# Gate and up projections of a feed-forward block by Strassen's seven half-size products

## The chip, the cores and the metric

One Trainium2 chip, one core. The metric is the device time of the whole program in microseconds. Before the change three runs gave 1579.23, 1581.88 and 1583.27 us, a median of 1581.88 us.

The engines are named as the profile names them: PE multiplies matrices, DVE and POOL do elementwise work, ACT does activations and copies, SP issues the DMAs. PE's accumulators lie in PSUM (tiles `pm`), everything else in SBUF.

## The reference

The program is a mixer block followed by a second transformer block over 512 tokens of width 1024, all in float32. The change touches the feed-forward at the end of the second block alone:

```python
h = rmsnorm(x, norm_ffn_pre[l])
f = (jax.nn.silu(h @ ffn_w_gate[l]) * (h @ ffn_w_up[l])) @ ffn_w_down[l]
x = x + rmsnorm(f, norm_ffn_post[l])
```

`h` is 512 x 1024, the gate and up weights are 1024 x 2816, that is 22 column tiles of 128, and the down weights are 2816 x 1024. To keep float32 accuracy each operand a is written as a high part (a rounded to fp32r) and a low part (a minus the high part, as fp32r), and a product of two operands is three matmuls: high by high, high by low, low by high.

## The kernel before, in words

The kernel records every operation with what it reads and writes, and a list scheduler (`Recorder.schedule`) then writes out one order for each engine from a table of durations, priorities (`key`, `boost`) and the counts of free buffers. At run time each engine goes through its list in order and waits on semaphores. Operations recorded with `either` may go to one of two engines, and the scheduler chooses: `copy` between ACT and DVE, `two` and `sub` between DVE and POOL, unless an operand lies in PSUM; those stay on DVE. All of them are issued through one helper line, so the profile shows line 439 for nearly everything and tiles tell the work apart.

The activations `h`, transposed, lie in two constants: high part `hbuf` and low part `hbuf_l`, written tile of 128 tokens by tile in `norm_tile`. In the profile both are `c`; in the order rows they are `c_84` (high) and `c_85` (low).

A projection with weights as the stationary operand is `proj_b`. For two column tiles (256 columns, 1 MB) `wunit` loads the weights into `wr` (two buffers), and for each column tile makes a high part `wh` with one `copy` of 128 x 1024 and a low part `wl` with one `sub` of 128 x 1024 (three buffers each, `NWH`). Then 8 slices of K times 3 matmuls of 512 tokens each add up in one PSUM tile: 24 matmuls for one column tile. The feed-forward loop takes two column tiles of gate and the same two of up, ten times with 512-token matmuls and once, first, with each split into two halves of 256 tokens (`FFH = 2`), so that the first halves can start before the norm of the last tokens is done. ACT takes the Silu of a gate tile out of PSUM, DVE multiplies it with the up tile in PSUM, and the result is split into parts for the down projection (`split`: a `copy` and a `sub` of 128 x 512).

In what follows a pair is one turn of that loop with 512-token matmuls: two column tiles of gate and the same two of up. Here are the changed functions and what calls them.

Of the kernel before, what the change touches and what calls it, by code (L numbers as in the profile page):

```python
# [10 lines left out]
F32 = mybir.dt.float32  # L11
F32R = mybir.dt.float32r
# [8 lines left out]
NT = 4  # L21
# [470 lines left out]
def body(ctx, tc, a, out, stop=None, probe=None):  # L492
# [142 lines left out]
    def proj_a(w, c0, n, act, consume, kt=KT, tail=4, boost=0):  # L635

        hh, hl = act
        ps = {}
        group = []
        for k0 in range(0, kt, 4):
            kn = min(4, kt - k0)
            rows = slice(k0 * 128, (k0 + kn) * 128)
            src = [w[rows, c:c + m] for c, m in c0] if isinstance(c0, list) else w[rows, c0:c0 + n]
            step = 1 if tail == kt else 2
            cuts = [slice(k, min(k + step, kn)) for k in range(0, kn, step)]
            parts = wunit(src, kn, n, [(k, slice(0, n)) for k in cuts], keep=(tail == kt))  # L650
            for cut, (wh, wl) in zip(cuts, parts):
                ks = [(k0 + k, wh[:, k - cut.start, :], wl[:, k - cut.start, :]) for k in range(cut.start, cut.stop)]
                group += ks
                if k0 + cut.stop > kt - tail and k0 + cut.stop < kt:
                    continue
                for t in range(NT):
                    ts = slice(t * 128, t * 128 + 128)
                    if t not in ps:
                        ps[t] = mmp()
                    for k, h_, l_ in group:  # L660
                        first, last = k == 0, k == kt - 1
                        T.matmul(ps[t][:, :n], hh[k][:, ts], h_, start=first, stop=False)
                        T.matmul(ps[t][:, :n], hh[k][:, ts], l_, start=False, stop=False)
                        T.matmul(ps[t][:, :n], hl[k][:, ts], h_, start=False, stop=last)
                    if group[-1][0] == kt - 1:
                        rec.boost = boost
                        consume(ps[t], t)
                        rec.boost = 0
                group = []

    def split(src, hi, lo):
        copy(hi, src)
        sub(lo, src, hi)
# [10 lines left out]
    def norm_tile(t, xa, xb, g):  # L684

        xns = [t2(), t2()]
        ssq = small([128, 2], tag="ssq", bufs=4)
        for c, xc in enumerate((xa, xb)):
            ACT.activation(xns[c], xc, AF.Square, accum_out=ssq[:, c:c + 1])
        rs = small([128, 1], tag="rstd", bufs=4)  # L690
        rsqrt(rs, ssq[:, 0:1], 1.0 / D, 1e-6, 1, ssq[:, 1:2])
        for c, xc in enumerate((xa, xb)):
            xn = xns[c]
            rec.either(lambda: ACT.activation(xn, xc, AF.Copy, scale=rs),
                       lambda: V.tensor_scalar(xn, xc, rs, None, op0=OP.mult))
            ps = mxp()
            for k in range(4):
                T.transpose(ps[:, k * 128:k * 128 + 128], xn[:, k * 128:k * 128 + 128], ident)
            f = t2()
            v3 = lambda ap: ap.rearrange("p (k n) -> p k n", k=4)  # L700
            two(OP.mult, v3(f), v3(ps), g[:, 4 * c:4 * c + 4][:, :, None].to_broadcast([128, 4, 128]))
            ts = slice(t * 128, t * 128 + 128)
            split(v3(f), hbuf[:, 4 * c:4 * c + 4, ts], hbuf_l[:, 4 * c:4 * c + 4, ts])


    sp.tile([128, 448], F32, tag="pad", name="pad", bufs=1)
# [1114 lines left out]
    def post_norm(name, src, done):  # L1821

        gb = [t2(), t2()]
        for c in range(2):
            load(gb[c], bcast_rows(a[name][0][c * 512:c * 512 + 512], 512))
        ssq = [small([128, 2], tag="psq", bufs=8) for _ in range(NT)]
        o = {}

        def make(c):
            def take(ps, t):  # L1830
                o[t, c] = t2()
                ACT.activation(o[t, c], ps, AF.Square, accum_out=ssq[t][:, c:c + 1])
# [14 lines left out]
    def mixed(t, x0, x1_):  # L1847
        for c, xc in enumerate((x0, x1_)):
            load(xd[1, t * 128:t * 128 + 128, c * 512:c * 512 + 512], xc)
        norm_tile(t, x0, x1_, g3_)  # L1850

    mk = post_norm("norm_mix_post_2", xd[0], mixed)
    for c in range(2):
        proj_a(a["w_out_2"][0], c * 512, 512, (mh, ml), mk(c), tail=TAIL2 if c else 4, boost=NBOOST * c)


    NF = 22
    fh, fl = [], []
    for j0 in range(0, NF, 2):
        sg_ = {}  # L1860

        def take_g(ps, j):
            sg_[j] = t2()
            ACT.activation(sg_[j], ps, AF.Silu)

        def take_up(ps, j):
            two(OP.mult, sg_[j], sg_[j], ps)
            fh.append(t2(F32R))
            fl.append(t2(F32R))
            split(sg_[j], fh[-1], fl[-1])  # L1870

        proj_b(a["ffn_w_gate_2"][0], j0 * 128, 256, hact, take_g, parts_of=2 if j0 < FFH else 1)
        proj_b(a["ffn_w_up_2"][0], j0 * 128, 256, hact, take_up, parts_of=2 if j0 < FFH else 1)

    def finish(t, x0, x1_):
        for c, xc in enumerate((x0, x1_)):
# [30 lines left out]
```

## Time and profile before

| | us |
|---|---|
| median of three runs | 1581.88 |
| the profiled execution's own time | 1583.61 |
| its span | 1581.8 |
| PE busy | 1475.5 (93%) |
| DVE busy | 1040.0 (66%) |
| ACT busy | 416.0 (26%) |
| POOL busy | 377.6 (24%) |

Busy shares are averages over stages with different limits. The feed-forward fills the last 370 us of the span: the two half-token tiles from about 1209 us, the ten pairs from about 1232 us to 1450 us, and the down projection with the last norm after that. In this stage the granted clock is 1.00, the upper of the two levels (2.4 GHz). Two things help in reading the rows below. An instruction's duration in the trace runs a little into the next one on the same engine, so the spacing of starts is the rate of an engine that is kept fed, and it is shorter than the duration. And an instruction that cannot get what it needs from the memory shows as a longer duration, not as an idle gap, so waits of that kind count as busy time.

### The profile page before, as it was taken

The numbers are of one execution on the slowest core, as the hardware profiler recorded it, in microseconds if no ns is written. First come the engines' busy times: TensorE is split into PE (matmuls) and PEld (weight loads), VectorE is DVE, ScalarE is ACT, GpSimd is POOL, SyncE is SP. The second block draws the span as 40 slices with busy tenths as digits, with TensorE's granted clock in tenths as the row PEclk, the third lists the DMA queues.
The fourth block names the chain that finished last, engine by engine and source line by source line (L and its number), as shares of the span: only waits on it lengthen the run. The fifth ranks groups of instructions, "written<-read, shape, count | busy, mean of one in ns | idle before, by whom it ended". The sixth has DMA issues, their size and how long they took to land.

```text
span 1581.8 us, 19335 instructions
## 1 busy us (share of the span) xinstructions
PE 1475.5 (93%) x7092; PEld 1210.0 (76%) x7092; DVE 1040.0 (66%) x2130; ACT 416.0 (26%) x905; POOL 377.6 (24%) x439
## 2 busy tenths in 40 slices
PE   6895988688999999989999999999999999999997
PEld 5674766577788887878887777778888888888886
DVE  5999995798874696696444777874478434443444
ACT  4351324344321132252011534431114111111010
POOL 2788741441200123020001221232120111110000
PEclk9997999899999999999999999999999999999999
DMA  8614232255613222213323223213343323333232
GB/s 235 203 40 156 82 79 51 67 149 180 213 49 127 62 78 83 81 35 99 106 81 120 94 67 105 69 54 106 118 151 118 106 88 99 107 96 104 81 133 107
DMA packets 169455, 165.26 MB, mean 104 GB/s; under 512 B 36992, under 2 KB 136200, under 8 KB 169232
## 3 DMA queue, kind: packets, MB, share of 16 engines
q1 hardware_dynamic: 169360, 164.02, 33.1%
q8 instruction: 56, 0.92, 0.2%
q14 instruction: 39, 0.32, 0.1%
HBM read 150.64 MB, written 10.47 MB: 102 GB/s over the span
## 4 chain that ended last, share of the span: by engine, by line
PE 65%; DVE 13%; DMA 2%; issue 2%; ACT 1%; POOL 1%; SPq 0%; DVEq 0%; ACTq 0%; POOLq 0%
PE pm L439 65%; DVE t L439 9%; DVE s L439 2%; DVE wl L439 1%; ACT t L439 1%; DMA wr<-w_in 1%; DMA wr<-w_ada 1%; POOL t L439 1%; DVE wh L439 1%; DVE c L439 0%; DMA t<-t 0%; SPq L439 0%; DMA t<-gla_w_alpha 0%; ACT L439 0%; ACT s L439 0%
## 5 line engine op out<-in xcount | busy, mean ns | idle before, releaser
L439 PE MATMUL pm<-c,wh 128*128 128x512 f32 (+1 forms) x1952 | 568.9, 388 | 4.5 <-DVE wh L439 2.5
L439 PEld LDWEIGHTS pm<-c,wh 128*128 128x128 f32 x1952 | 359.1, 189 | 75.5 <-DVE wh L439 3.4
L439 POOL TENSOR_TENSOR t<-t,t 128x512 f32<-128x512 f32 (+11 forms) x282 | 261.7, 941 | 627.7 <-ACT t L439 421.2
L439 DVE CAST wh<-wr 128x1024 fp32r<-128x1024 f32 x160 | 113.9, 712 | 356.4 <-PE pm L439 344.2
L439 PE MATMUL pm<-c,wl 128*128 128x512 f32 (+1 forms) x976 | 325.5, 387 | 0.6 <-DVE wl L439 0.5
L439 ACT ACTIVATE t<-pm 128x512 f32<-128x512 f32 (+8 forms) x315 | 150.1, 502 | 510.9 <-PE pm L439 488.0
L439 PE MATMUL pm<-t,t 128*128 128x256 f32 (+4 forms) x1232 | 242.3, 324 | 30.9 <-DVE t L439 18.2
L439 DVE TENSOR_TENSOR wl<-wr,wh 128x1024 fp32r<-128x1024 f32 (+2 forms) x195 | 244.1, 1255 | 24.3 <-PE pm L439 9.3
L439 PEld LDWEIGHTS pm<-t,t 128*128 128x128 f32 (+1 forms) x1232 | 193.7, 191 | 62.8 <-issue 14.2
L439 PEld LDWEIGHTS pm<-c,wl 128*128 128x128 f32 x976 | 183.1, 189 | 36.8 <-DVE wl L439 1.4
L439 PE MATMUL pm<-wh,c 128*128 128x512 f32 (+1 forms) x576 | 177.6, 391 | 4.0 <-DVE wh L439 2.5
L439 PE MATMUL pm<-c,t 128*128 128x128 f32 (+4 forms) x638 | 123.7, 307 | 30.9 <-DVE t L439 14.7
L439 PE MATMUL pm<-wh,t 128*128 128x512 f32 x480 | 142.2, 390 | 0.3 <-POOL t L439 0.3
L439 ACT ACTIVATE t<-t 128x512 fp32r<-128x512 f32 (+6 forms) x140 | 79.0, 581 | 229.2 <-DVE t L439 168.3
L439 PE MATMUL pm<-t,wh 128*128 128x512 f32 x416 | 137.2, 391 | 0.0
L439 PEld LDWEIGHTS pm<-c,t 128*128 128x128 f32 (+3 forms) x638 | 82.8, 152 | 64.2 <-issue 16.2
L439 PEld LDWEIGHTS pm<-wh,c 128*128 128x128 f32 x576 | 108.3, 192 | 26.9 <-DVE wh L439 3.2
L439 POOL TENSOR_TENSOR wl<-wr,wh 128x1024 fp32r<-128x1024 f32 (+1 forms) x17 | 42.7, 2513 | 320.6 <-DVE wh L439 200.6
L439 PE MATMUL pm<-wl,c 128*128 128x512 f32 (+1 forms) x288 | 104.6, 394 | 15.0 <-DVE wl L439 15.0
L439 ACT ACTIVATE wh<-wr 128x1024 fp32r<-128x1024 f32 (+2 forms) x52 | 52.9, 1019 | 203.9 <-PE pm L439 149.6
L439 PEld LDWEIGHTS pm<-wh,t 128*128 128x128 f32 x480 | 90.0, 188 | 20.0 <-POOL t L439 0.7
L439 DVE TENSOR_TENSOR t<-pm,t 64x256 f32<-64x256 f32 (+8 forms) x157 | 85.2, 557 | 24.8 <-ACT t L439 17.8
(113 smaller groups left out, 1346.4 us busy)
## 6 DMA issues: line engine op xcount, KB each, us to landing
wr<-w_in SPq DMA_DIRECT2D x48, 1024.0 KB, 5.0
wr<-w_branch SPq DMA_DIRECT2D x12, 1024.0 KB, 5.2
wr<-ffn_w_gate SPq DMA_DIRECT2D x11, 1024.0 KB, 5.2
wr<-ffn_w_up SPq DMA_DIRECT2D x11, 1024.0 KB, 5.2
wr<-ffn_w_down SPq DMA_DIRECT2D x10, 1024.0 KB, 5.0
wa<-w_ada SPq DMA_DIRECT2D x32, 256.0 KB, 4.3
wr<-w_out SPq DMA_DIRECT2D x8, 1024.0 KB, 4.9
wr<-w_in SPq DMA_DIRECT2D x12, 512.0 KB, 3.8
```

The lines of the kernel that those rows point to most:

```text
L439: self.rec.record(self.eng, lambda: fn(*args, **kw), writes, reads, self.duration(name, writes, reads, kw))
```

## The change

For 20 of the 22 column tiles (all but the first two) the product of 1024 x 256 weights with 512 tokens is split into 2 x 2 blocks: K in halves of 512, columns in halves of 128, tokens in halves of 256. Seven products of half-size blocks (Strassen, in Winograd's form) replace eight. Each of the seven has a stationary operand of 4 slices of K by 128 columns and a moving operand of 256 tokens, and is again three matmuls for each slice of K: 7 x 4 x 3 = 84 matmuls of 256 tokens for two column tiles instead of 48 of 512.

Of the weight blocks, four combinations are formed in place in `wr` (`two`, 128 x 512 each), and each of the seven operands gets its own high and low part, both in one tile (`block`: a `copy` and a `sub` of 128 x 512). Of the activations, four combinations with their parts are formed once (`combine`, called after the half-token tiles). The seven products come back from PSUM through seven DVE operations that add them up. The product of Silu(gate) and up, `glu_half`, is now of two SBUF tiles, and its split into parts is recorded after all pairs.

```diff
+    def block(src):
+        tag = ("wh", "wl")[blocks[0] % 2]
...
+        hi, lo = (t[:, c:c + 512].rearrange("p (k n) -> p k n", k=4) for c in (0, 512))
+        copy(hi, src)
+        sub(lo, src, hi)
...
+        def product(o, wp_, b):
+            for k in range(4):
+                T.matmul(o, wp_[0][:, k, :], b[k][0], start=(k == 0), stop=False)
+                T.matmul(o, wp_[0][:, k, :], b[k][1], start=False, stop=False)
+                T.matmul(o, wp_[1][:, k, :], b[k][0], start=False, stop=(k == 3))
...
+            w11 = block(a11)
+            product(x[:, lo_], w11, b11)
+            two(OP.subtract, a21, a11, a21)
+            ws3 = block(a21)
+            two(OP.subtract, a21, a22, a21)
+            ws2 = block(a21)
+            two(OP.add, a11, a11, a21)
+            ws1 = block(a11)
+            product(y[:, lo_], ws3, t3)
+            product(x[:, hi_], ws2, t2_)
+            product(y[:, hi_], ws1, t1)
+            w12 = block(a12)
+            w22 = block(a22)
+            two(OP.subtract, a12, a12, a21)
+            ws4 = block(a12)
+            product(z[:, lo_], w12, b21)
+            product(z[:, hi_], w22, t4n)
+            product(q[:, lo_], ws4, b22)
+            copy(o[:, lo_], x[:, lo_])
+            V.tensor_tensor(m[:, lo_], o[:, lo_], x[:, hi_], op=OP.add)
+            V.tensor_tensor(m[:, hi_], m[:, lo_], y[:, lo_], op=OP.add)
+            V.tensor_tensor(h2(p), h2(m), y[:, None, hi_].to_broadcast([128, 2, 256]), op=OP.add)
+            V.tensor_tensor(o[:, lo_], o[:, lo_], z[:, lo_], op=OP.add)
+            V.tensor_tensor(o[:, hi_], m[:, hi_], z[:, hi_], op=OP.add)
+            V.tensor_tensor(p[:, lo_], p[:, lo_], q[:, lo_], op=OP.add)
...
-        proj_b(a["ffn_w_gate_2"][0], j0 * 128, 256, hact, take_g, parts_of=2 if j0 < FFH else 1)
-        proj_b(a["ffn_w_up_2"][0], j0 * 128, 256, hact, take_up, parts_of=2 if j0 < FFH else 1)
...
+            proj_s(a["ffn_w_gate_2"][0], j0 * 128, 256, hact, comb, take_g2)
+            proj_s(a["ffn_w_up_2"][0], j0 * 128, 256, hact, comb, lambda os, j: [glu_half(sg_[z], os[z]) for z in range(2)])
```

The scheduler settles the order on each engine. In the middle of the ten pairs DVE's list before reads as follows; `wr_2436` and `wr_2445` are the raw weights of one pair's gate and up, and these ten rows are the whole pair:

```order
L439 CAST wh_2437<-wr_2436 128x1024
L439 TENSOR_TENSOR wl_2438<-wr_2436,wh_2437 128x1024
L439 CAST wh_2439<-wr_2436 128x1024
L439 TENSOR_TENSOR t_2422<-t_2422,pm_2430 128x512
L439 TENSOR_TENSOR wl_2440<-wr_2436,wh_2439 128x1024
L439 CAST wh_2446<-wr_2445 128x1024
L439 TENSOR_TENSOR t_2424<-t_2424,pm_2433 128x512
L439 TENSOR_TENSOR wl_2447<-wr_2445,wh_2446 128x1024
L439 CAST wh_2448<-wr_2445 128x1024
L439 TENSOR_TENSOR wl_2449<-wr_2445,wh_2448 128x1024
```

After the change a pair has 35 rows on DVE, and the same 35 come back pair by pair. These twelve are a third of one pair (`wr_2466` is its gate, `wr_2481` its up; `wh_2467` is the operand w11 of the gate, `wh_2473`, `wl_2474` and `wh_2477` are ws2, ws1 and ws4; `pm_2453` to `pm_2456` are the products of the unit before):

```order
L439 TENSOR_TENSOR wr_2466<-wr_2466 128x4x128
L439 TENSOR_TENSOR t_2465<-t_2465,pm_2454 128x256
L439 TENSOR_TENSOR wh_2467<-wr_2466,wh_2467 128x512
L439 TENSOR_TENSOR t_2464<-t_2465,pm_2454 128x512
L439 TENSOR_TENSOR wr_2466<-wr_2466 128x4x128
L439 TENSOR_TENSOR wr_2481<-wr_2481 128x4x128
L439 CAST wh_2477<-wr_2466 128x512
L439 TENSOR_TENSOR t_2463<-t_2463,pm_2455 128x256
L439 TENSOR_TENSOR wh_2477<-wr_2466,wh_2477 128x512
L439 TENSOR_TENSOR wh_2473<-wr_2466,wh_2473 128x512
L439 TENSOR_TENSOR wl_2474<-wr_2466,wl_2474 128x512
L439 TENSOR_TENSOR t_2463<-t_2465,pm_2455 128x256
```

The whole 35 are 18 operations of two SBUF inputs on 128 x 512 (combinations of weights, low parts, one product with Silu, one low part of the result), 4 casts of 128 x 512, 2 sums of 128 x 512 and 10 of 128 x 256 with one input in PSUM, and one copy of 128 x 256 out of PSUM.

On POOL a pair had two rows before, the low parts of two result tiles. These are two pairs and a half:

```order
L439 TENSOR_TENSOR t_2432<-t_2422,t_2431 128x512
L439 TENSOR_TENSOR t_2435<-t_2424,t_2434 128x512
L439 TENSOR_TENSOR t_2452<-t_2442,t_2451 128x512
L439 TENSOR_TENSOR t_2455<-t_2444,t_2454 128x512
L439 TENSOR_TENSOR t_2472<-t_2462,t_2471 128x512
```

After the change it has eight: three combinations of weights, three low parts of weight blocks, one product with Silu and one low part of a result:

```order
L439 TENSOR_TENSOR wr_2466<-wr_2466 128x4x128
L439 TENSOR_TENSOR wh_2475<-wr_2466,wh_2475 128x512
L439 TENSOR_TENSOR wr_2466<-wr_2466 128x4x128
L439 TENSOR_TENSOR wl_2476<-wr_2466,wl_2476 128x512
L439 TENSOR_TENSOR t_2448<-t_2448,t_2463 128x512
L439 TENSOR_TENSOR wh_2487<-wr_2481,wh_2487 128x512
L439 TENSOR_TENSOR t_2691<-t_2449,t_2690 128x512
L439 TENSOR_TENSOR wr_2481<-wr_2481 128x4x128
```

All eight read two SBUF tiles. ACT has 15 rows in a pair where it had four: eleven high parts of weight blocks, two Silu, one copy out of PSUM and one high part of a result. On PE the operand w11 of a unit is taken between the last two products of the unit before: the order of a boundary is (`wh_2461` and `wl_2462` are w22 and ws4 of the unit before)

```order
L439 MATMUL pm_2455<-t_2365,wh_2461 128x256
L439 MATMUL pm_2468<-c_84,wh_2467 128x256
L439 MATMUL pm_2468<-c_85,wh_2467 128x256
L439 MATMUL pm_2455<-t_2364,wh_2461 128x256 x2
L439 MATMUL pm_2455<-t_2365,wh_2461 128x256
L439 MATMUL pm_2456<-c_84,wl_2462 128x256
L439 MATMUL pm_2455<-t_2364,wh_2461 128x256
L439 MATMUL pm_2468<-c_84,wh_2467 128x256 x2
```

## Rows read from the trace of the kernel before

**Rows 1.** The page: span, and busy time of each engine with its instructions.
```profile
span 1581.8 us, 19335 instructions
PE 1475.5 (93%) x7092; PEld 1210.0 (76%) x7092; DVE 1040.0 (66%) x2130; ACT 416.0 (26%) x905; POOL 377.6 (24%) x439
```

**Rows 2.** The chain that ended last: start, us, what; the feed-forward's stretch.
```profile
1209.34 9.40 PE pm L439 x77
1218.79 0.64 PE pm L439 x4
...
1221.59 349.64 PE pm L439 x1595
1571.25 0.70 ACT t L439 x2
```

**Rows 3.** Busy time in stretches: us, engines (instructions), granted clock, DMA share, GB/s.
```profile
1254.00:1276.00 22.00, 22.00 (x99) 18.21 (x98) 8.87 (x10) 2.46 (x4) 3.08 (x2) 1.00 0.32 96
1364.00:1386.00 22.00, 22.00 (x99) 18.22 (x98) 8.87 (x10) 2.46 (x4) 3.08 (x2) 1.00 0.30 96
```

**Rows 4.** PE in order of time, start and us: 512-token matmuls late in the pairs.
```profile
1441.51 0.61 PE L439 MATMUL pm<-c,wh 128*128 128x512 f32 x2
...
1449.24 0.39 PE L439 MATMUL pm<-c,wl 128*128 128x512 f32 x1
```

**Rows 5.** PE in order of time: 256-token matmuls of the half-token tiles.
```profile
1210.03 0.40 PE L439 MATMUL pm<-c,wh 128*128 128x256 f32 x2
...
1213.51 0.40 PE L439 MATMUL pm<-c,wh 128*128 128x256 f32 x2
```

**Rows 6.** DVE in order of time, undisturbed: 512 columns, 256 out of PSUM, a cast.
```profile
411.95 0.42 DVE L439 CAST t<-wr 128x512 fp32r<-128x512 f32 x1
412.33 4.05 DVE L439 TENSOR_TENSOR t<-wr,t 128x512 fp32r<-128x512 f32 x3
...
538.53 0.42 DVE L439 TENSOR_TENSOR t<-pm,t 128x256 f32<-128x256 f32 x1
538.87 0.42 DVE L439 BATCH_NORM_STATS2 s<-pm 128x6 f32<-128x256 f32 x1
...
1208.60 0.68 DVE L439 TENSOR_TENSOR c<-t,c 128x512 fp32r<-128x512 f32 x1
1209.20 0.68 DVE L439 TENSOR_TENSOR t<-pm,c 128x512 f32<-128x512 f32 x1
```

**Rows 7.** DVE in order of time, where POOL works at the same time.
```profile
860.93 1.28 DVE L439 SCALAR_TENSOR_TENSOR t<-t,pm 128x512 f32<-128x512 f32 x2
...
1079.11 1.22 DVE L439 TENSOR_TENSOR wl<-wr,wh 128x1024 fp32r<-128x1024 f32 x1
1080.73 1.83 DVE L439 TENSOR_TENSOR wl<-wr,wh 128x1024 fp32r<-128x1024 f32 x1 [0.40 <-ACT wh L439]
...
1162.89 1.63 DVE L439 CAST wh<-wr 128x1024 fp32r<-128x1024 f32 x1
```

**Rows 8.** POOL in order of time, in the same moments, and back to back.
```profile
123.10 4.62 POOL L439 TENSOR_TENSOR t<-t,t 128x512 f32<-128x512 f32 x4
...
859.90 3.26 POOL L439 TENSOR_TENSOR wl<-wr,wh 128x1024 fp32r<-128x1024 f32 x1 [0.69 <-PE pm L439]
...
1079.28 2.20 POOL L439 TENSOR_TENSOR t<-t,t 128x512 f32<-128x512 f32 x1 [13.82 <-DVE t L439]
...
1161.83 2.13 POOL L439 TENSOR_TENSOR t<-t,t 128x512 f32<-128x512 f32 x1 [12.52 <-DVE t L439]
```

**Rows 9.** Groups by form from 1230 to 1440 us: count, busy us, mean ns.
```profile
L439 DVE TENSOR_TENSOR wl<-wr,wh 128x1024 fp32r<-128x1024 f32 x38 | 46.5, 1223 | 1.9
L439 POOL TENSOR_TENSOR t<-t,t 128x512 fp32r<-128x512 f32 x20 | 30.4, 1519 | 229.0 <-ACT t L439 229.0
...
L439 ACT ACTIVATE t<-t 128x512 fp32r<-128x512 f32 x20 | 12.7, 633 | 107.3 <-DVE t L439 107.3
```

More of the change, by code (lines that the diff above doesn't have):

```diff
@@ L656, in proj_a @@
                 for t in range(NT):
-                    ts = slice(t * 128, t * 128 + 128)
+                    tok = lambda x: x[t] if isinstance(x, list) else x[:, t * 128:t * 128 + 128]
                     if t not in ps:
@@ L661, in proj_a @@
                         first, last = k == 0, k == kt - 1
-                        T.matmul(ps[t][:, :n], hh[k][:, ts], h_, start=first, stop=False)
-                        T.matmul(ps[t][:, :n], hh[k][:, ts], l_, start=False, stop=False)
-                        T.matmul(ps[t][:, :n], hl[k][:, ts], h_, start=False, stop=last)
+                        T.matmul(ps[t][:, :n], tok(hh[k]), h_, start=first, stop=False)
+                        T.matmul(ps[t][:, :n], tok(hh[k]), l_, start=False, stop=False)
+                        T.matmul(ps[t][:, :n], tok(hl[k]), h_, start=False, stop=last)
                     if group[-1][0] == kt - 1:
@@ new lines, in combine @@
+    def combine(f):
+        tiles = [[(t2(F32R), t2(F32R)) for _ in range(2)] for _ in range(4)]
+        v3 = lambda ap: ap.rearrange("p (k n) -> p k n", k=4)
+        for q in range(2):
+            t1, t2_, t3, t4n = (t2() for _ in range(4))
+            two(OP.subtract, t1, f[q + 2][0], f[q][0])
+            two(OP.subtract, t3, f[q + 2][1], f[q + 2][0])
+            two(OP.subtract, t2_, f[q + 2][1], t1)
+            two(OP.subtract, t4n, f[q][1], t2_)
+            for z, src in enumerate((t1, t2_, t3, t4n)):
+                for kp in range(2):
+                    hi, lo = (x.rearrange("p (k n) -> p k n", k=2)[:, :, q * 128:q * 128 + 128] for x in tiles[z][kp])
+                    split(v3(src)[:, 2 * kp:2 * kp + 2, :], hi, lo)
+        return [[tuple(x[:, k % 2 * 256:k % 2 * 256 + 256] for x in z[k // 2]) for k in range(4)] for z in tiles]
@@ L686, in norm_tile @@
         xns = [t2(), t2()]
+        fs = []
         ssq = small([128, 2], tag="ssq", bufs=4)
@@ L703, in norm_tile @@
             split(v3(f), hbuf[:, 4 * c:4 * c + 4, ts], hbuf_l[:, 4 * c:4 * c + 4, ts])
+            fs.append(f)
+        return fs
     sp.tile([128, 448], F32, tag="pad", name="pad", bufs=1)
@@ L1849, in mixed @@
             load(xd[1, t * 128:t * 128 + 128, c * 512:c * 512 + 512], xc)
-        norm_tile(t, x0, x1_, g3_)
+        ftok[t] = norm_tile(t, x0, x1_, g3_)
+    ftok = {}
     mk = post_norm("norm_mix_post_2", xd[0], mixed)
@@ L1857, in body, with glu_half @@
     NF = 22
-    fh, fl = [], []
+    ff = []
+    def glu_half(g, u):
+        two(OP.mult, g, g, u)
+        ff.append(g)
     for j0 in range(0, NF, 2):
@@ L1864, in take_g, with take_g2, f_slices @@
             ACT.activation(sg_[j], ps, AF.Silu)
[L1866 to L1870, printed above, removed]
-        proj_b(a["ffn_w_gate_2"][0], j0 * 128, 256, hact, take_g, parts_of=2 if j0 < FFH else 1)
-        proj_b(a["ffn_w_up_2"][0], j0 * 128, 256, hact, take_up, parts_of=2 if j0 < FFH else 1)
+        def take_g2(os, j):
+            for z, o in enumerate(os):
+                ACT.activation(o, o, AF.Silu)
+                sg_[z] = o
+        if j0 < FFH:
+            proj_b(a["ffn_w_gate_2"][0], j0 * 128, 256, hact, take_g, parts_of=2)
+            proj_b(a["ffn_w_up_2"][0], j0 * 128, 256, hact, lambda ps, j: glu_half(sg_[j], ps), parts_of=2)
+            if j0 + 2 == FFH:
+                comb = combine(ftok)
+        else:
+            proj_s(a["ffn_w_gate_2"][0], j0 * 128, 256, hact, comb, take_g2)
+            proj_s(a["ffn_w_up_2"][0], j0 * 128, 256, hact, comb, lambda os, j: [glu_half(sg_[z], os[z]) for z in range(2)])
+    fp = []
+    for f in ff:
+        fp.append((t2(F32R), t2(F32R)))
+        split(f, *fp[-1])
+    def f_slices(x):
+        res = []
+        for j in range(NF):
+            if j < FFH:
+                res.append([fp[j][x][:, t * 128:t * 128 + 128] for t in range(NT)])
+            else:
+                res.append([fp[j - j % 2 + t // 2][x][:, j % 2 * 256 + t % 2 * 128:j % 2 * 256 + t % 2 * 128 + 128]
+                            for t in range(NT)])
+        return res
+    fh, fl = f_slices(0), f_slices(1)
     def finish(t, x0, x1_):
```

26 lines of the change are left out of this document (added).

## The prediction

> **What bounds the kernel now.** I read the page first, then the chain of waits, then stretches of the feed-forward, then single instructions in order of time.
>
> The page has PE busy in 93% of a span of 1581.8 us, DVE in 66%, ACT and POOL in about a quarter [rows 1]. The chain says more: from 1221.59 to 1571 us it is PE alone, 1595 matmuls without a link through another engine [rows 2]. So in the stage that the change touches PE sets the end, and what PE saves there is saved. The stretches agree: in 22 us, which is about one pair of gate and up, PE is busy for 22.00, DVE for 8.87, POOL for 3.08, ACT for 2.46, at a granted clock of 1.00, the upper level [rows 3]. The reader should see how much room DVE and POOL have there; the question is whether the change needs more than that room.
>
> **The change part by part.**
>
> *PE.* Late in the pairs 34 matmuls of 512 tokens start between 1441.51 and 1449.24 us, 0.227 us each [rows 4]. The half-token tiles have 29 matmuls of 256 tokens between 1210.03 and 1213.51 us, 0.120 us each, with the same 128 x 128 stationary operands [rows 5]. So half the tokens cost a little more than half. Removed are 20 x 48 = 960 of the first kind, 217.9 us; added are 20 x 84 = 1680 of the second, 201.6 us. PE's own saving is 16.3 us, not the eighth of 218 that counting multiplications would give. In pairs: 96 x 0.227 = 21.8 us before, 168 x 0.120 = 20.2 us after.
>
> The Trainium skill, "TensorE: Matmul & The Clock Gate", section "Back-to-back issue gap", gives a warm isolated gap of N/2.4 + 2.5 ns, 216 and 109 ns here. By that the saving would be 960 x 0.216 - 1680 x 0.109 = 24 us, an estimate from the page; the trace has 227 and 120 ns, which decide.
>
> *DVE.* Undisturbed and kept fed, a two-input operation of 128 x 512 starts 0.60 us before the next (1208.60 to 1209.20), one of 128 x 256 out of PSUM 0.34 (538.53 to 538.87), a cast of 128 x 512 0.38 (411.95 to 412.33) [rows 6]. The 35 rows of a pair are then 18 x 0.60 = 10.8 (two SBUF inputs), 4 x 0.38 = 1.5 (casts), 2 x 0.60 = 1.2 and 11 x 0.34 = 3.7 (out of PSUM), together 17.2 us where there were 8.9. By itself this fits into 20.2 us of PE.
>
> *POOL.* A pair has eight operations of 128 x 512 instead of two. Four back to back take 4.62 us [rows 8], under 1.2 us each; eight are some 9 us. This fits too.
>
> *Both together.* They cannot run at the same time. At 1079.28 us POOL starts an operation 0.17 us into a DVE subtraction that takes its usual 1.22 us to 1080.33; POOL's takes 2.20, to 1081.48: it waited for DVE and then ran for 1.15. The next DVE subtraction starts at 1080.73 and takes 1.83 instead of 1.22, because POOL was still at work for 0.75 [rows 7 to 9]. The cast at 1162.89 lost even more, 1.63 us beside a POOL operation that ended at 1163.96. Only the two DVE operations at 860.93 with an input in PSUM keep to 0.64 each, in the middle of a POOL operation of 3.26 us [rows 7, 8]. So each POOL operation of 128 x 512 blocks a DVE operation with two SBUF inputs, or an SBUF cast, for 1.0 to 1.1 us, and is blocked by it in turn.
>
> The Trainium skill, "SBUF — State Buffer", section "Who interferes with whom", states the same as a rule: DVE's second read port is GpSimd's, the pair of ports is an exclusive lock held for the whole instruction, and a DVE instruction with at most one SBUF input outside the two-port modes does not take it. It speaks against this change, which puts both engines on that lock; the trace agrees with it, at 1.22 against 1.83 us and at 0.64 us undisturbed.
>
> The sum for the lock in a pair: 10.8 + 1.5 us of DVE and 8 x 1.0 to 1.1 us of POOL, 20.3 to 21.1 us. This is as long as PE's 20.2 even when the 4.9 us of DVE work out of PSUM lies entirely beside POOL. It won't, since DVE runs its list in order. Where a POOL operation gets in beside one operation of 0.34 us, DVE loses 0.65 us.
>
> A second limit: the operand ws4 of a unit takes the buffer of w11 of the same unit (every second operand has the same tag, three buffers). The order has the cast of ws4 three rows behind w11's low part, and it waits until PE has finished w11, which stands interleaved with the last two products of the unit before. From w11's first low part PE has about 25 matmuls to go, 3.0 us, and 0.2 us for the signals; the three rows between are 1.8 us. So DVE idles for 1.4 us twice in a pair, 2.8 us. During these idles and the row out of PSUM beside them four of the eight POOL operations can run for nothing (their inputs are ready then). The other four cost 4 x 0.65 = 2.6 us. An operation started afresh takes 0.68 instead of 0.60 us, eight times, 0.6 us. Together 17.2 + 2.8 + 2.6 + 0.6 = 23.2, and I take 23.3 us for a pair, 1.5 more than before, 15 us in ten pairs. The bounds are 20.2 (PE alone, -16) and 26 us (17.2 and eight holds of 1.1 that nothing hides, +42).
>
> *The start.* Four combinations of the activations and their parts need eight subtractions of 128 x 512 and sixteen casts and subtractions each of 128 x 256, about 8 x 0.6 + 16 x 0.7 = 16 us spread over three engines, in the time in which before DVE finished the norm of the last tokens and PE waited for it (from 1218.79 to 1221.59 us in the chain [rows 2]). POOL takes six of the early ones, in the midst of DVE's chain of small operations for that norm. I charge 2 us for the norm and 3 us for the second up tile of the half-token stage, whose weights DVE now prepares behind nineteen other rows: 5 us, bounds 0 and 10.
>
> *What costs nothing.* ACT goes from 4 to 15 operations in a pair, 15 x 0.63 = 9.5 us [rows 9], below any of the others. The weights loaded are the same megabyte for each unit, at a DMA share of 0.3 [rows 3]. The down projection and the last norm keep their work; the parts of the results are made one pair later than before, well ahead of use.
>
> The sum against the profiled execution, 1583.6 us: + 15 + 5 = 1603.6. That execution lay 1.7 us above the median of the runs, so I predict 1602 us; alone this case has 1592 to 1614.
>
> **The rivals.**
>
> *PE stays the bound.* It needs DVE and POOL to pass the lock back and forth almost without loss, 20.2 us in a pair. For it: each of the engines alone has room, and six operands can be ready ahead of PE. Against it: the lock alone needs at least as long. The time: 1583.6 - 16.3 + 2 - 1.7 = 1568 us. (By the page's gaps on PE it would be 8 us less.)
>
> *The lock, well packed.* POOL's operations all meet DVE's idle time or its work out of PSUM: a pair of 21.1 to 21.8 us, -7 to 0 us in ten, with 3 to 5 us at the start: about 1580 us. For it: DVE has 4.9 us out of PSUM and 2.8 us idle for POOL's 8 to 8.8 us. Against it: POOL's operations become ready together, after the same DVE row.
>
> *The lock, badly packed.* Nearly every hold falls on DVE, and PE's late products then hold up DVE's sums: a pair of 25 to 26 us, +32 to +42, with 5 to 8 at the start: about 1626 us. The point from which it decides is DVE without idle time and POOL waiting on DVE's last row, which three of its eight operations do by their inputs.
>
> **How the numbers follow.** My forecast has a chance of 0.60, PE as the bound 0.13, the well packed lock 0.13, the badly packed 0.14. A change under 0.3% (4.7 us) can't be told from none. Faster by more: all of the PE case and a little of the well packed one, 0.15. Within: most of the well packed one, 0.10. Slower: the rest, 0.75. The range is 1572 to 1628 us: it leaves out most of the PE case and the upper end of the badly packed one, and holds the bounds of the start.
>
> **What would show it.** In the stretch of the pairs PE should be busy for less than nine tenths where it had no idle time, with its waits on DVE's and POOL's low parts (`wh`, `wl`); DVE should be busy for over nine tenths; its subtractions of 128 x 512 beside POOL should average over 0.8 us where those out of PSUM stay at 0.69; ten pairs should take some 233 us. Idle PE under 3% in the pairs, or subtractions that keep to 0.69 us beside POOL, would prove the lock harmless and me wrong. If the first pair starts at the time it did before, the 5 us for the start are wrong.

## The result: 2.97% slower, and the profile after

The changed kernel takes 1629.32 us (median of four runs, 1624.83 to 1631.36) where the kernel before, run beside it, takes 1582.14 us: a ratio of 1.0297 with an interval of 1.0271 to 1.0323. The forecast was 1602 us with a range of 1572 to 1628. Its direction was right, and so was the cause that it named, DVE and POOL shutting each other out; the step by which half of POOL's operations cost nothing failed, and the change cost 47 us in place of 20. Times here and below are medians of the fast runs, without one slow run each of e6 and e8. In the profiled execution the page has, as answer to [rows 1] (span; busy time, share and instructions of each engine):

```profile
span 1626.5 us, 21349 instructions
PE 1477.3 (91%) x7812; PEld 1240.4 (76%) x7812; DVE 1207.3 (74%) x2396; ACT 483.8 (30%) x1025; POOL 487.5 (30%) x513
```

No engine looks full here: a page is a mean over stages. The second stretch of [rows 3], and a longer one that is used below to compare kernels (us; each engine's busy time and instructions; granted clock; DMA share; GB/s):

```profile
1364.00:1386.00 22.00, 19.03 (x151) 18.22 (x152) 21.36 (x30) 6.90 (x13) 11.55 (x8) 1.00 0.32 98
...
1270.00:1410.00 140.00, 117.86 (x923) 112.39 (x923) 136.16 (x193) 48.38 (x83) 67.09 (x45) 0.99 0.27 83
```

PE, which was busy for 22.00 of 22 us, is now busy for 19.03; DVE went from 8.87 to 21.36. Over 140 us DVE is busy for 97% and PE for 84%: the bound has moved to DVE. DVE's list for one pair, from one first eviction (`COPY t<-pm`) to the next, in order of time (start, duration, instruction, and in brackets what ended an idle time before it):

```profile
1340.96 0.41 DVE L439 COPY t<-pm 128x256 f32<-128x256 f32 x1
1341.30 0.67 DVE L439 TENSOR_TENSOR wl<-wr,wl 128x512 fp32r<-128x512 f32 x1
...
1343.16 1.73 DVE L439 TENSOR_TENSOR wh<-wr,wh 128x512 fp32r<-128x512 f32 x1
1344.81 0.67 DVE L439 TENSOR_TENSOR t<-t,pm 128x512 f32<-128x512 f32 x1
1345.41 1.78 DVE L439 TENSOR_TENSOR wr<-wr 128x512 f32<-128x512 f32 x2
1347.82 0.43 DVE L439 CAST wh<-wr 128x512 fp32r<-128x512 f32 x1 [0.63 <-PE pm L439]
...
1350.96 1.68 DVE L439 TENSOR_TENSOR wl<-wr,wl 128x512 fp32r<-128x512 f32 x1
1352.57 1.78 DVE L439 TENSOR_TENSOR t<-t,t 128x512 f32<-128x512 f32 x1
...
1355.87 1.45 DVE L439 TENSOR_TENSOR wr<-wr 128x512 f32<-128x512 f32 x1
...
1357.84 1.77 DVE L439 TENSOR_TENSOR wh<-wr,wh 128x512 fp32r<-128x512 f32 x1
1359.54 1.77 DVE L439 TENSOR_TENSOR wr<-wr 128x512 f32<-128x512 f32 x1
...
1363.70 1.77 DVE L439 TENSOR_TENSOR wh<-wr,wh 128x512 fp32r<-128x512 f32 x1
...
1366.39 0.41 DVE L439 COPY t<-pm 128x256 f32<-128x256 f32 x1
```

And POOL's list for the same time, in the same columns:

```profile
1343.05 1.29 POOL L439 TENSOR_TENSOR wr<-wr 128x512 f32<-128x512 f32 x1 [3.56 <-DVE wr L439]
1344.29 1.75 POOL L439 TENSOR_TENSOR wl<-wr,wl 128x512 fp32r<-128x512 f32 x1
1350.79 1.30 POOL L439 TENSOR_TENSOR t<-t,t 128x512 f32<-128x512 f32 x1 [4.75 <-DVE t L439]
1352.30 1.50 POOL L439 TENSOR_TENSOR wh<-wr,wh 128x512 fp32r<-128x512 f32 x1 [0.20 <-ACT wh L439]
1355.09 1.68 POOL L439 TENSOR_TENSOR t<-t,t 128x512 fp32r<-128x512 f32 x1 [1.29 <-ACT t L439]
1357.39 3.37 POOL L439 TENSOR_TENSOR wr<-wr 128x512 f32<-128x512 f32 x2 [0.63 <-DVE wr L439]
1363.58 1.34 POOL L439 TENSOR_TENSOR wh<-wr,wh 128x512 fp32r<-128x512 f32 x1 [2.81 <-ACT wh L439]
```

A pair takes 25.43 us (1340.96 to 1366.39). The rows at 1341.30 and 1344.81 show what a two-input operation of 128x512 takes when nothing blocks it, 0.67 to 0.68 us. Eight rows are longer, each beside one of POOL's eight operations: by 1.05, 0.50 (1.78 for two instead of 1.28), 1.00, 1.10, 0.77, 1.09, 1.09 and 1.09 us, together 7.7 us, 0.96 each. Such a lengthening is called a hold below. DVE is idle once, for 0.63 us. The rest, 25.43 - 7.7 - 0.63 = 17.1 us, is DVE's own work. The row at 1344.81 reads PSUM and runs at 0.67 us in the midst of a POOL operation (1344.29 to 1346.04).

The pair is 25.43 - 21.8 = 3.6 us longer than before, 36 us in ten pairs. The rest of the 47 us is lost at the start, in the half-token tiles. Executions differ by a few us ahead of the changed stage already, so the start is counted from a mark in the unchanged part, PE's 5300th matmul (it starts at 1188.07 us before and 1186.71 after), to the first matmul on gate and up weights behind the 192 of the half-token tiles (1236.85 and 1245.27): 48.8 us before, 58.6 after, 9.8 lost. From there to the end of the span it is 345.0 and 381.3 us, 36.3 more. DVE in the norm of the last tokens:

```profile
1214.90 0.16 DVE L439 SCALAR_TENSOR_TENSOR s<-s,s 128x1 f32<-128x1 f32 x1
...
1216.38 0.87 DVE L439 SCALAR_TENSOR_TENSOR s<-s,s 128x1 f32<-128x1 f32 x1
...
1217.78 1.25 DVE L439 SCALAR_TENSOR_TENSOR s<-s 128x1 f32<-128x1 f32 x1
```

POOL at that time, six subtractions of the token combinations in a row:

```profile
1215.95 7.20 POOL L439 TENSOR_TENSOR t<-t,t 128x512 f32<-128x512 f32 x6 [7.06 <-DVE t L439]
```

And PE, which waits for the norm's result:

```profile
1223.58 1.37 PE L439 MATMUL pm<-c,t 128*128 128x128 f32 x8 [4.56 <-DVE t L439]
1225.68 1.01 PE L439 MATMUL pm<-c,wh 128*128 128x256 f32 x3 [0.74 <-ACT c L439]
1228.33 0.58 PE L439 MATMUL pm<-c,wh 128*128 128x256 f32 x1 [1.64 <-DVE c L439]
...
1234.26 0.37 PE L439 MATMUL pm<-c,wl 128*128 128x256 f32 x1
```

A row of one column, 0.16 us when free, takes 0.87 and 1.25 us beside POOL, and the norm is a chain of such rows; rows of the combinations stand between them in DVE's own list too. PE goes on with the last tokens at 1228.33 us; before it was at 1221.59 [rows 2], 6.7 us earlier. After these waits 27 matmuls of 256 tokens start between 1228.33 and 1234.26, 0.220 us each in place of 0.120 [rows 5], 2.7 us more, with the granted clock at its lower level, 0.50, for four of the microseconds:

```profile
1229.00:1233.00 4.00, 4.00 (x21) 4.00 (x21) 4.00 (x7) 0.72 (x2) 2.93 (x3) 0.50 0.01 4
...
1245.00:1253.00 8.00, 6.04 (x45) 5.84 (x44) 6.53 (x7) 2.31 (x4) 3.81 (x3) 0.91 0.08 19
```

The second line is the first Strassen tile, where PE is idle for another 2.0 us; that lies inside the first pair, which takes 25.2 us, no longer than the others, and is not a loss of the start. The late resumption (6.7 us, 8.1 by the mark) and the lower clock (2.7 us) are the 9.8 us of the start to within 1 us.

### The profile page after: what moved, and what is told of

It is laid out like the page before. It is cut to its first block, busy times and chain, and to the rows that moved or that the text cites. A ratio compares the mean times of both kernels' runs of the same rounds, so it can differ in the third digit from the quotient of the medians.

```text
span 1626.5 us, 21349 instructions
## 1 busy us (share of the span) xinstructions
PE 1477.3 (91%) x7812; PEld 1240.4 (76%) x7812; DVE 1207.3 (74%) x2396; ACT 483.8 (30%) x1025; POOL 487.5 (30%) x513
## 4 chain that ended last, share of the span: by engine, by line
PE 53%; DVE 24%; issue 3%; DMA 2%; POOL 1%; ACT 1%; SPq 0%; DVEq 0%; ACTq 0%; POOLq 0%
PE pm L439 53%; DVE t L439 13%; DVE wl L439 4%; DVE wh L439 3%; DVE s L439 2%; POOL t L439 1%; DVE wr L439 1%; ACT t L439 1%; DMA wr<-w_in 1%; DMA wr<-w_ada 1%; DVE c L439 1%; DMA t<-t 0%; SPq L439 0%; DMA t<-gla_w_alpha 0%; POOL wh L439 0%
## 5 line engine op out<-in xcount | busy, mean ns | idle before, releaser
L439 PE MATMUL pm<-c,wh 128*128 128x512 f32 (+1 forms) x1672 | 484.4, 368 | 15.2 <-DVE wh L439 11.0
L439 PEld LDWEIGHTS pm<-c,wh 128*128 128x128 f32 x1672 | 303.3, 192 | 63.5 <-DVE wh L439 13.7
L439 DVE CAST wh<-wr 128x1024 fp32r<-128x1024 f32 (+1 forms) x132 | 92.2, 699 | 230.1 <-PE pm L439 220.8
L439 PE MATMUL pm<-t,wh 128*128 128x256 f32 (+1 forms) x896 | 234.2, 334 | 2.0 <-DVE wh L439 2.0
L439 PE MATMUL pm<-t,wl 128*128 128x256 f32 (+1 forms) x688 | 170.4, 319 | 6.5 <-DVE wl L439 6.5
L439 ACT ACTIVATE wh<-wr 128x512 fp32r<-128x512 f32 (+1 forms) x110 | 89.4, 814 | 281.9 <-PE pm L439 224.9
L439 PEld LDWEIGHTS pm<-t,wh 128*128 128x128 f32 x896 | 155.0, 191 | 19.5 <-DVE wh L439 3.2
L439 ACT ACTIVATE t<-t 128x512 f32<-128x512 f32 (+6 forms) x162 | 89.3, 572 | 161.6 <-DVE t L439 96.3
L439 PEld LDWEIGHTS pm<-t,wl 128*128 128x128 f32 x688 | 117.8, 193 | 16.0 <-DVE wl L439 8.0
L439 DVE TENSOR_TENSOR t<-t,t 128x512 f32<-128x512 f32 (+8 forms) x174 | 124.8, 729 | 7.0 <-DMA t<-t 2.1
```

Of the source, the lines that this page charges most:

```text
L439: self.rec.record(self.eng, lambda: fn(*args, **kw), writes, reads, self.duration(name, writes, reads, kw))
```

## The experiments

The texts set apart, written before each run, say TensorE, VectorE, GpSimd and ScalarE for PE, DVE, POOL and ACT. The theory at the beginning: each of the eight POOL operations of a pair locks DVE out for some 0.97 us, and this makes DVE the bound at 25.4 us. Rival A: DVE is held up by PE, which gives weight blocks back too late (the step with 2.8 us of idle time in the prediction). Rival B: PE's stream of 256 tokens is slower than was charged.

A pair is 168 matmuls, so matmuls in the stretch from 1270 to 1410 us give the pair: 923 of them are 25.5 us (and 25.43 from eviction to eviction). Ratios are to the kernel before, run beside it.

| version | POOL operations a pair | pair, us | time, us | ratio |
|---|---|---|---|---|
| changed kernel | 8 | 25.5 | 1629.3 | 1.0297 (1.0271 to 1.0323) |
| e1 ScalarE copies in place of POOL | 0 | 20.1 | 1576.3 | 0.9971 (0.9958 to 0.9985) |
| e2 more POOL | 12 | 26.3 | 1642.0 | 1.0382 (1.0363 to 1.0401) |
| e3 DVE alone | 0 | 20.1 | 1579.8 | 0.9988 (0.9979 to 0.9998) |
| e4 combinations off POOL | 8 | 25.8 | 1621.9 | 1.0250 (1.0233 to 1.0267) |
| e6 e3 and e4 | 0 | 20.8 | 1575.3 | 0.9971 (0.9960 to 0.9983) |
| e7 e6 and norm first | 0 | 20.6 | 1571.7 | 0.9950 (0.9938 to 0.9963) |
| e8 half of POOL's | 4 | 24.3 | 1606.8 | 1.0167 (1.0151 to 1.0182) |
| e9 e7 and casts on ScalarE | 0 | 20.1 | 1566.6 | 0.9915 (0.9902 to 0.9929) |
| e10 holds alone | 4 | 23.2 | 1606.7 | 1.0161 (1.0144 to 1.0178) |
| e11 e8, four blocks | 5 | 21.0 | 1589.5 | 1.0056 (1.0041 to 1.0071) |
| e12 changed, four blocks | 10 | 24.0 | 1617.8 | 1.0224 (1.0204 to 1.0244) |

### e1: the same lists, without POOL

Operations recorded within the pairs and the splits of their products are marked (`zone`); the planner's order stays.

```diff
+        rec.ops[-1].subst = lambda: nc.scalar.activation(dst, a_, AF.Copy)      # in two()
...
-                op.call()
+                (op.subst if op.zone and op.subst and op.eng == "POOL" else op.call)()
```

> In the twenty Strassen tile pairs and the splits of their products, each two-input operation that GpSimd had (about 83, eight in a gate-and-up pair) is replaced by a ScalarE copy of its first input, so the weight differences and low parts that GpSimd made are not computed; VectorE and TensorE run the same lists as in the changed kernel. Theory (the lock on SBUF between VectorE and GpSimd makes VectorE the bound, eight holds of 0.97 us a pair): the pair falls from 25.4 to 20.2 to 20.6 us, where TensorE is next (VectorE's own 35 rows are 17.2), and the time to 1577 to 1584 us. Rival A (VectorE waits for TensorE to give back weight blocks, whatever GpSimd does): only the 0.6 us idle a pair and a little latency go, pair above 24, time 1610 to 1625. Rival B (TensorE's 256-wide stream is slower than the 0.120 us charged): pair 22 to 24, time 1595 to 1615.

The stretch 1270 to 1410 us in its trace:

```profile
1270.00:1410.00 140.00, 140.00 (x1169) 140.00 (x1168) 120.63 (x243) 88.42 (x159) 0.00 (x0) 1.00 0.33 103
```

PE is busy for all of the 140 us, 0.120 us a matmul: rival B falls, PE's term of the prediction is right. The pair and the time (1576.3 us) came out just under the theory's ranges. The groups by form in 1260 to 1420 us (count; busy us, mean ns; idle time before them and what ended it) show DVE's rows free of stalls, and its waits for PE:

```profile
L441 DVE TENSOR_TENSOR wh<-wr,wh 128x512 fp32r<-128x512 f32 x39 | 26.1, 685 | 0.4
...
L441 DVE CAST wl<-wr 128x512 fp32r<-128x512 f32 x16 | 6.8, 427 | 11.6 <-PE pm L441 11.6
...
L441 DVE CAST wh<-wr 128x512 fp32r<-128x512 f32 x8 | 3.4, 426 | 9.4 <-PE pm L441 9.4
```

The first of these groups in the changed kernel, between 1270 and 1410 us:

```profile
L439 DVE TENSOR_TENSOR wh<-wr,wh 128x512 fp32r<-128x512 f32 x28 | 35.8, 1297 | 0.0
```

Its mean falls from 1297 to 685 ns. DVE waits 21.0 us for PE in 160 us, 2.6 us a pair. That is the idle time which the prediction put at 2.8. It is there when PE is the bound and nothing blocks DVE.

### e3: GpSimd taken out, arithmetic whole

```diff
-        if not any(in_psum(view(x)) for x in (dst, a_, b_)):
+        if not rec.zone and not any(in_psum(view(x)) for x in (dst, a_, b_)):      # in two(): no POOL in the pairs
```

> The same arithmetic, with GpSimd taken out of the pairs: its eight operations go to VectorE. Theory (lock): VectorE has 17.2 + 8 x 0.60 = 22.0 us of rows a pair and no stalls; pair 22.0 to 22.6, time 1629 - 31 = 1598 us (1594 to 1604). Rival A (VectorE is late by its own work and by waits for TensorE): eight more rows on the bound engine, pair 25.4 + 4.8 = 30, time 1677; Rival B (TensorE's stream): pair stays at 24 to 25.4, time 1615 to 1630.

```profile
1270.00:1410.00 140.00, 140.00 (x1169) 140.00 (x1169) 137.70 (x262) 73.08 (x129) 0.00 (x0) 1.00 0.33 104
```

DVE has more to do than in the changed kernel, 19.8 us a pair in place of 17.1, and the pair became 5.3 us shorter: rival A in its form "DVE has too much to do" is out. With e1, where the lists are the same, it is POOL's part that costs the time; e10 below separates its holds from its slowness. The size was missed by 18 us. The pair is not 22.0 us but PE's 20.1, because the planner made another list. In the groups from 1260 to 1420 us DVE has nine casts of weights, about one a pair in place of three, and only two of the subtractions that split the products, which are put off until after the pairs:

```profile
L441 DVE CAST wl<-wr 128x512 fp32r<-128x512 f32 x5 | 2.1, 424 | 0.1
L441 DVE CAST wh<-wr 128x512 fp32r<-128x512 f32 x4 | 1.7, 425 | 0.1
L441 DVE TENSOR_TENSOR t<-t,t 128x512 fp32r<-128x512 f32 x2 | 1.4, 684 | 0.0
```

DVE has 137.70 us of 140 to do, just less than PE. In all the kernel is within 0.3% of the one before: what the pairs win (16 us) is lost again outside them. By the mark the start takes 57.9 us in place of 48.8, 9.1 of it; where the down projection begins PE stands for another 1.95 us (1453.76 to 1455.71), waiting for `wh`.

### e4, e6, e7, e9: the start

e4 keeps the pairs as they are and takes POOL out of the combinations alone; e6 is e3 and e4; e7 also lets no combination start before the norm of all tokens; e9 also puts every cast in the pairs and combinations on ACT.

```diff
+                rec.zone = True                     # e4, e6, e7, e9
+                rec.after = tuple(normed)           # e7, e9: all operations of the norm come first
                 comb = combine(ftok)
+                rec.after = ()
...
+        if rec.zone:                                # e9, in copy()
+            ACT.activation(dst, src, AF.Copy)
+            return
```

> Only the token combinations ahead of the pairs are kept off GpSimd (their differences and low parts run on VectorE); the pairs are as in the changed kernel. Theory (the start's 7 us comes from GpSimd's holds on the small VectorE rows of the last tokens' norm): the last tokens' c_85 is ready some 4 us earlier, VectorE has some 3 us more of its own work, time 1622 to 1628 us. Rival (the combinations themselves are late, whoever does them): same or later, 1629 to 1633.

> GpSimd is kept off both the pairs and the token combinations; the arithmetic is whole. Theory (two separate costs of the same lock, the pairs' and the start's): the gains of the two single edits add, 1580 - 7 = 1573 us (1570 to 1576), pair 20.16 us as TensorE sets it. Rival (with the pairs bound by TensorE the start's gain is lost again, since VectorE has the combinations to do itself): 1577 to 1582.

> As the run before, and the combinations may start only when the norm of all four token tiles is done. Theory (VectorE's order at the start, combinations between the small rows of the last norm, keeps TensorE waiting for the last tokens): TensorE resumes at about 1218 us in place of 1222 to 1225, time 1569 us (1565 to 1572). Rival (the combinations are then late for the first pair, which waits for them): 1573 to 1580.

> As the norm-first version, with every cast of the pairs and combinations on ScalarE (before, the planner chose VectorE for some). Theory (TensorE is the bound at 20.16 us a pair, and VectorE at 19.8 has just enough room): VectorE falls to some 19 us a pair and the time stays within 2 us of the norm-first version. Rival (VectorE still holds TensorE back here and there): 3 to 6 us faster than that version.

e4 won 7.5 us, a little more than was expected. PE goes on with the last tokens at 1221.75 us, 6.6 us earlier; 2.0 of that lie ahead of the stage (the 5300th matmul starts at 1184.76). By the mark the start takes 54.4 us in place of 58.6, so POOL's holds there cost 4.2 of the 9.8 us, net of the work that DVE took over.

e6 came to 1575.3, near the upper end of what the two gains added give. e7 won another 3.7 us, resumes with the last tokens at 1219.89 us and came to 1571.7, inside its range; by the mark its start takes 48.8 us, as in the kernel before. Of the other 5.6 of the start's 9.8 us, 1.9 go with POOL out of the pairs too (e6, 52.5 us) and 3.7 when the combinations no longer stand ahead of the norm's last rows in DVE's list.

In e6 and e7 PE is not quite full in the pairs: 1129 and 1144 matmuls between 1270 and 1410 us make 20.8 and 20.6 us a pair. In e6 that is a single pair of 25.0 us, with a wait of 2.31 us for DVE and a granted clock of 0.78 from 1385 to 1390 us behind it; in e7 each pair from 1316 us on takes 20.7 to 20.8.

e9 has 1169 and 20.1, so its expectation (within 2 us of e7) failed and its rival held, with 5 us. That it was the casts that held PE back in e7 is not shown: DVE is as busy in e9 (138.37 us of 140, against 138.06) and did not fall to some 19 us a pair, since the planner gave it other rows in their place. How close DVE may come to PE depends on the order. The stretch of e9:

```profile
1270.00:1410.00 140.00, 140.00 (x1169) 140.00 (x1168) 138.37 (x258) 75.74 (x139) 0.00 (x0) 1.00 0.34 106
```

Its chain of waits (start, us, what) is PE alone from the last tokens on, where e7's still has links through DVE:

```profile
1221.68 333.55 PE pm L441 x2315
```

e9 is the best version of the study: 1566.6 us (1565.99 to 1567.61), a ratio of 0.9915 (0.9902 to 0.9929). The gain, 13.4 us by the medians, is PE's term of the prediction, 16.3 us, with little lost. (The profiled spans differ by 16.0, of which 2.6 lie ahead of the stage.)

### e2, e8, e10: the price of one hold

e2 adds 42 POOL products of 128x448, four a pair, that nobody needs. e8 replaces every second of POOL's operations as in e1. e10 replaces all, and adds 42 products of 128x512 on POOL that read finished parts and whose result nobody needs.

```diff
+                if op.zone and op.eng == "POOL":                               # e2
+                    count += 1
+                    if count % 2:
+                        nc.gpsimd.tensor_tensor(spare, ones[:, :448], ones[:, :448], op=OP.mult)
...
-                op.call()
+                mine = op.zone and op.subst and op.eng == "POOL"               # e8
+                count += bool(mine)
+                (op.subst if mine and count % 2 else op.call)()
...
+                if mine and not op.made.tensor.name.startswith("wr"):          # e10, after op.subst() for all
+                    held += 1
+                    if held % 4:
+                        nc.gpsimd.tensor_tensor(shaped(spare), op.made, shaped(ones), op=OP.mult)
```

> The changed kernel with 42 more GpSimd products of 128x448 (two a tile pair, four in a gate-and-up pair) that read a constant and write a spare tile which nobody reads. Theory (lock): every one of them holds VectorE for about 0.9 us more, 3.7 us a pair; pair 29, time about 1629+37=1666 us (1655 to 1675). Rivals A and B: GpSimd is idle more than half of the pair, so nothing or at most 5 us: 1629 to 1634.

> In the pairs every second of GpSimd's two-input operations (some 42, four in a gate-and-up pair) is replaced by a ScalarE copy of its first input, so that part of the weight differences and low parts is not computed; GpSimd keeps the other half. Theory (each hold costs VectorE about 0.97 us, none hidden): VectorE 17.0 + 4 x 0.97 + 0.4 = 21.2 us a pair, time 1576 + 11 = 1587 us (1583 to 1592). Rival (what the prediction reckoned: four holds a pair fall into VectorE's waits for TensorE and cost nothing): the pair stays at 20.2, time 1576 to 1580.

> All of the pairs' GpSimd operations are replaced by ScalarE copies of their first input (weight differences and low parts that GpSimd made are not computed), and 42 GpSimd products of 128x512 that read a finished low part or product and write a spare tile nobody reads are added, four in a gate-and-up pair: as many holds as with half of the operations left on GpSimd, but no result of GpSimd in the chain from weight to product. Theory (the holds themselves cost the time): pair 23 to 24.5 us, time 1603 to 1610. Rival (it is GpSimd's 1.5 us in place of 0.6 in the chain that makes the weight blocks that cost the time): pair 20.2 to 21, time 1576 to 1583.

Three kernels, the stretch 1270 to 1410 us. e2:

```profile
1270.00:1410.00 140.00, 117.26 (x894) 113.25 (x894) 136.13 (x185) 46.20 (x79) 88.48 (x63) 0.95 0.24 77
```

e8:

```profile
1270.00:1410.00 140.00, 125.10 (x968) 121.24 (x968) 122.00 (x203) 61.73 (x109) 33.23 (x23) 0.96 0.27 85
```

e10:

```profile
1270.00:1410.00 140.00, 127.83 (x1013) 124.99 (x1012) 125.12 (x211) 76.72 (x138) 31.16 (x22) 0.98 0.29 91
```

Two of three expectations of the theory failed, in opposite ways. Four holds more than eight cost 12.7 us (1642.0 against 1629.3), not 37. Four holds cost 30.5 us more than none (1606.8 against 1576.3), not 11, and eight cost 53. So the price is not a constant that is added to DVE's work. e10 has e8's price with no result of POOL in the chain of weights (1606.7 us; 23.2 against 24.3 us a pair with 22 and 23 operations in the stretch, 23.1 against 23.5 over the first nine pairs): it is mainly the holds and not POOL's slowness that cost the time. A part of the difference between their pairs may be that slowness.

Why e2's extra holds were cheap is seen in part in DVE's rows of e2:

```profile
1347.82 1.72 DVE L441 TENSOR_TENSOR wh<-wr,wh 128x512 fp32r<-128x512 f32 x1
1349.47 0.68 DVE L441 TENSOR_TENSOR t<-t,pm 128x512 f32<-128x512 f32 x1
1350.07 2.52 DVE L441 TENSOR_TENSOR wr<-wr 128x512 f32<-128x512 f32 x2
```

and POOL's:

```profile
1347.71 1.29 POOL L441 TENSOR_TENSOR wr<-wr 128x512 f32<-128x512 f32 x1 [2.29 <-DVE wr L441]
1348.96 1.74 POOL L441 TENSOR_TENSOR wl<-wr,wl 128x512 fp32r<-128x512 f32 x1
1350.65 1.38 POOL L554 TENSOR_TENSOR pad<-c 128x448 f32<-128x448 f32 x1
```

POOL's third operation follows its second at once, and the two engines take turns: DVE gets one row in between two of POOL's, and here the extra operation adds only 0.74 us (the two rows take 2.52 instead of the changed kernel's 1.78). Over the whole stretch DVE's rows are longer by 8.5 us a pair than the same rows of e1, where the changed kernel's are by 7.6 (estimates from the means of the groups), for 3.5 operations more, and DVE is idle for 0.7 us in both. Where each of the others went was not followed.

Why e8's holds were dear is seen in its groups, 1260 to 1420 us:

```profile
L441 DVE TENSOR_TENSOR wl<-wr,wl 128x512 fp32r<-128x512 f32 x39 | 38.4, 997 | 0.0
...
L441 DVE CAST wl<-wr 128x512 fp32r<-128x512 f32 x12 | 5.1, 425 | 10.8 <-PE pm L441 6.5 <-issue 4.3
...
L441 DVE CAST wh<-wr 128x512 fp32r<-128x512 f32 x7 | 3.0, 428 | 7.6 <-PE pm L441 7.6
```

The subtractions are held (a mean of 997 ns; some 1.0 us for each POOL operation over all groups), and still DVE is idle before its casts for 18.4 us, 2.8 a pair, as in e1, 14.1 of it for PE, although PE is no longer full: it is busy for 125.10 of 140 us, and its longest waits from 1260 to 1420 us (us in total, times, longest) are for DVE's weights:

```profile
PE pm L441 <- DVE wl L441: 11.8, 7, 2.0
```

Neither engine is the bound. The reading is that a hold makes a weight part late and PE stands; then PE gives a block back late, and DVE stands; e11 tests it. The idle time is not a reserve that pays for the holds.

### e11, e12: more blocks between the two engines

```diff
-NSLOT = 58
+NSLOT = 54
-NWH = 3
+NWH = 4          # e11: in e8; e12: in the changed kernel
```

> The half-holds version (every second GpSimd operation of the pairs a ScalarE copy, that part not computed) with four weight blocks of each kind in place of three, and four fewer 128x512 tiles in the common pool to make room. Theory (TensorE and VectorE wait for each other in turn, because three blocks let VectorE run too little ahead, so that a hold is not made up for out of VectorE's 3 us of idle time a pair): the pair falls from 24.1 to 21.2 to 22.5 us, time 1607 - 20 = 1580 to 1595. Rival (blocks are not what couples them): the pair stays at 24 and the time within 5 us of 1607, or later if the smaller pool costs something elsewhere.

> The changed kernel, all its arithmetic, with four weight blocks of each kind in place of three and four fewer tiles in the common pool. Theory (with all eight holds VectorE is the bound by its sum, 17.1 us of rows and 7.7 us of stalls, and only its 0.6 us idle can be won): pair 24.4 to 25.4 us, time 1620 to 1630. Rival (the three blocks cost as much here as with half of the holds): pair 21 to 23, time 1585 to 1605.

e11:

```profile
1270.00:1410.00 140.00, 135.46 (x1121) 134.44 (x1120) 136.54 (x222) 71.89 (x126) 50.04 (x33) 1.00 0.32 99
```

e12:

```profile
1270.00:1410.00 140.00, 125.67 (x980) 124.32 (x979) 139.18 (x193) 48.73 (x84) 87.86 (x58) 0.94 0.29 91
```

With four blocks e8's pair falls from 24.3 to 21.0 us, with even more POOL operations (33 in place of 23), and the time by 17 us: with three blocks PE and DVE stand in turn, with four they hardly do. In e12 DVE is busy for 139.18 of 140 us and the pair is still 24.0 (expected 24.4 to 25.4; the time was 2 us below its range): with all the holds DVE's sum is the bound, and more blocks win its last idle time and about 1 us a pair of work that the planner moved to POOL (ten operations a pair; an estimate from the means of the groups). Both carry a reservation: the planner knows the sizes, so its order and POOL's share changed too, and the pool of tiles is smaller. Both edits hold for the whole program, and time is lost with them ahead of the stage already: PE's 5300th matmul starts at 1194.44 us in e11 and 1200.56 in e12, against 1183.87 in e8 and 1186.71 in the changed kernel. So the two times show less than what four blocks win in the pairs.

## Why the prediction was wrong

**PE's term** was right: 20.2 us a pair was forecast, 20.1 measured in e1, e3 and e9.

**DVE's own work** was right: 17.2 us forecast, 17.1 measured. So was the number of POOL's operations, eight.

**The price of a hold** was right in its largest value (1.0 to 1.1 us forecast, 1.00 to 1.10 in six of eight rows) and wrong where it was used. The step that failed is "During these idles and the row out of PSUM beside them four of the eight POOL operations can run for nothing", and with it "The other four cost 4 x 0.65 = 2.6 us". All eight hit a DVE row, for 0.96 us on average: 7.7 in place of 2.6. The reason given, that their inputs are ready in the idles, was wrong: DVE's one idle, at 1347.2 us, has no POOL operation in it. Three of POOL's shown rows wait for a DVE row (`<-DVE wr`, `<-DVE t`), three for an ACT copy (`<-ACT wh`, `<-ACT t`) and one follows at once, and each starts 0.1 to 1.1 us ahead of a DVE row with two SBUF inputs (1343.05 against 1343.16, 1363.58 against 1363.70, 1344.29 against 1345.41). e8 tests the step directly: with only four operations the pair goes from 20.1 to 24.3 us (23.5 over the first nine pairs).

**The idle time** of 2.8 us a pair was put in as a fixed part of DVE's list, beside the holds. As a size it was right for a pair that PE bounds (e1: 2.6 us), though no row shows the 0.2 us for signals in it by themselves. With eight holds DVE is the later one, and 0.63 us is left. In between, with four, it stays and the holds come on top (e8). So a wait for another engine need not stay what it is in another state of the loop. The sum that would have held is 17.1 + 7.7 + 0.6 = 25.4 us, which was the rival "the lock, badly packed" (25 to 26 us a pair, about 1626 us, chance 0.14). Ten pairs cost 36 us, not 15: 21 of the 27 us by which the forecast was short.

**The start** cost 9.8 us in place of 5, at the upper end of its bounds of 0 to 10: 5 of the other 6 us. The norm had been charged 2 us for six POOL operations in the midst of DVE's small rows; PE resumed 6.7 us later, since a row of one column can be held for as long (1.09 us) as one of 512 (1.10), and since the combinations that DVE had itself stood ahead of the norm's last rows (3.7 us by e7). The lower clock after PE's waits, 2.7 us, was not in the list at all. The last 1 us is within what executions differ by ahead of the stage.

**What ACT and the loads would cost**, nothing, was right: ACT is busy for 48.38 of 140 us, and the DMA share is 0.27.

**What would show it** was mostly as written: PE below nine tenths (84%), DVE above (97%), its subtractions beside POOL at a mean of 861 to 1297 ns, the ones out of PSUM at 674. PE's waits were for DVE's parts and ACT's, and for none of POOL's. Ten pairs took 254 us by the pair shown, not 233.

The rule in the Trainium skill, "SBUF — State Buffer", section "Who interferes with whom", that the shared ports are locked for a whole instruction, agrees with the traces here: DVE's subtractions keep to 683 to 686 ns in e1 and e3, where POOL is out of the pairs, and rows with an input in PSUM keep to 0.67 us beside POOL.

## What to carry to other kernels

Before a second engine is given a share of the elementwise work, ask whether the two can run at the same time at all: here VectorE alone, with ScalarE for the casts, does the same pairs in 20.1 us (e3) for which VectorE and GpSimd together need 25.4. In this loop of two engines with few buffers between them idle time was no reserve: four holds in each of ten pairs cost 30.5 us (e8) although VectorE was idle for 2.8 us in each, and the sum has to be made for the state in which the loop ends, not for the one seen before. And a chain of tiny operations is a bad neighbour for long locks and for bulk work in the same list: with GpSimd out and the bulk work moved behind the norm the start took 48.8 us again in place of 58.6 (e7).

## What the runs showed of the hardware

- A VectorE row of one column and two SBUF inputs, 0.16 us when free, took 0.87 and 1.25 us beside six GpSimd subtractions of 128x512 back to back.
- The price of a hold on the time ran from 0.3 us (e2, 42 on top of eight a pair: 12.7 us) to 0.7 (e8, four a pair in place of none: 30.5 us for some 42), while VectorE's rows were longer by 0.7 and 1.0 us for each GpSimd operation (estimates from the means of the groups against those of e1).
- After PE had waited 4.56, 0.74 and 1.64 us with eight small transposes and three matmuls between, its granted clock was at the lower level, 1.2 GHz (0.50 from 1229 to 1233 us), and its matmuls came every 0.220 us in place of 0.120, until 1234.
